# Filler projections of the last four attention phases: no bound on how early they issue, shares by key blocks at 1.25 times the even rate, and all value rows of the second pair before head 2's long blocks

## The chip, the cores and the metric

The kernel runs on one core of a Trainium2 chip. Its time is the device time of one execution in microseconds (us); lower is better. The engines that matter here are TensorE (PE, with its weight loads, PEld), VectorE (DVE), ScalarE (ACT), GpSimd (POOL) and SyncE (SP), whose queue issues every DMA of this kernel.

## What is computed

One decoder layer in fp32 on x of 1024 tokens by 1024 features. Two attention groups share an input projection: a differential group of 4 heads and a sparse group of 8 heads (compressed, selected and windowed keys, mixed by gates). Their results are concatenated, projected, added to the scaled residual and normalized; a SwiGLU feed-forward layer with a second residual and normalization follows. The part that the change concerns is the differential group:

```python
s = jnp.einsum('bqhcd,bkhcd->bhcqk', q_blk, k) * scale - slopes * dist   # c = 0, 1: two maps per head
p = masked_softmax(s, dist >= 0)                                        # causal
a = p[:, :, 0] - lam * p[:, :, 1]
o = einsum('bhqk,bkhe->bqhe', a, v)                                     # 128 columns per head
o = rms_norm(o, subln_g) * (1.0 - lam_init)
mix = concatenate([o_diff, o_nsa]) @ w_out
x = layer_norm(alpha * x + mix)
```

## The kernel before

Tokens are cut into 8 blocks of 128 (NB), features into 8 tiles of 128 (KT). Large products keep fp32 accuracy with three matmuls each (`mm3`, lines 116 to 118): high and low parts of either operand, hi*hi, hi*lo, lo*hi. A loaded weight is split into these parts by ACT (line 81) and DVE or POOL (line 83). PSUM has 8 banks: `psM` 2 for projections, `psS` 2 for scores, `psT` 3 for transposes, `psO` 1 for outputs.

A **unit** is one block of 128 queries of one head; below, d2.7 is head 2, block 7, of the differential group. `diff_units` gives each unit a `front` and a `back`. The front runs, for both maps, the scores on PE (lines 331 and 334, in pieces of at most 512 keys), a fused bias-and-minimum on DVE that takes them out of PSUM (line 340) and the exponential on ACT (line 354); then DVE (lines 475 to 478) and POOL (lines 480 and 481) combine the two maps. The back transposes the combined map on PE (line 363), copies it by ACT (line 366), multiplies by the values (line 493) and takes the block's output out by DVE and ACT (lines 497 and 498). When four blocks of a half are done, `finish` scales their rows (lines 506 to 510, with a power on POOL at 509), transposes (line 513) and stores them to `mix_d` in DRAM (line 518). Blocks 0 to 3 are a head's first half, 4 to 7 its second. Block i sees i + 1 key blocks, so blocks 4 to 7 are the long ones.

**Fillers** are projections that PE runs beside the attention, each a generator with a step for every feature tile (three matmuls): `qdf(h, hf)` and `kdf(h, hf)` project queries and keys of head h for a half of the tokens (512 columns, 24 matmuls; called QDh.hf and KDh.hf below), `dvf(pair, blocks)` the value rows of a pair of heads (256 columns, 24 matmuls for each block of 128 tokens), `out_fill(i)` the output projection of token block i (two halves of 24 matmuls in two `psM` banks). A projected query half is taken out by ACT and DVE (lines 176 and 177) into two `q` tiles of four, and three DMA moves (line 161), the third after the first two, put its parts on the other partitions. Weights stand in `w` tiles, five buffers. `wo_fill(nh)` loads half of the output weights into the buffers of x (`big` tiles, free once the projections of that half of x have run), eight loads of 256 KB with eight splits on ACT and POOL. `out_start(i)` loads the residual rows and the block's `mix_d` rows; the sparse heads' feature tiles come first in the accumulation, the differential heads' last. `held_fill` and `out_fill` thus wait for the first half of all four differential heads.

What sets the order: the program is traced once with a priority for every instruction, and a scheduler with a timeline of its own then fixes each engine's order ahead of the run; on the chip each engine takes its instructions in that order. Fillers are traced at a priority 2000 behind (`FILL_LATER`). The **planner** (line 858 on) goes through `phases`. A phase has units, fillers, `look` (how many fronts run ahead of their backs), `ahead` (a factor on the filler rate), `later` (a priority delay of the backs) and `passed`. While a back is traced, `pump` traces filler steps until the phase's `due` is reached; `share` says how much of the fillers a unit gets, from the planner's estimates of PE and DVE work in `work`. What a phase leaves over is traced in a burst at its end. With `passed` n, `proj_mm3` (line 312 on) orders each projection matmul on PE behind the first score matmul that stands n + 1 marks back in `marks`; every map of every unit sets one mark. With `None` there is no such order.

Filler order in the last four phases before, worked out from the table and the estimates: KD3.0, KD3.1, QD3.0 beside d1.7, d2.0 and d2.1; QD2.1 and value rows 4 and 5 of pair 1 beside d2.2, d2.3, d3.0, d3.1; value rows 6 and 7 and QD3.1 beside d3.2 and d3.3; output blocks 0 and 1 beside d2.4 and d2.5; output blocks 2 and 3 beside the rest. Value row 5 is traced after the front of d3.3.

Of the kernel before, what the change touches and what calls it, by code (L numbers as in the profile page):

```python
# [37 lines left out]
def layer_kernel(ctx: ExitStack, tc: tile.TileContext, xT, x, w_t, w_vg, w_dv, lam_in, subln,  # L38
# [105 lines left out]
    with ExitStack() as ctx_a:  # L144
# [238 lines left out]
        def nsa_units(p, qt, K, V):  # L383
# [7 lines left out]
            def make(i, kind):  # L391
# [55 lines left out]
                n = -(-cols // 512)  # L447
                pe = n * streamed(cols / n, 4) + streamed(P, 2 * nb + 2 * (1 - kind)) + streamed(256, 2 * nb + 1 - kind)
                dve = 2 * row_ops(width, n) + nb // 2 * 0.69 + nb % 2 * 0.42 + (0.58 if kind else 1.19)
                return front, back, (pe, dve)  # L450

            return [make(i, kind) for i in range(NB) for kind in range(2)]

# [2 lines left out]
        def diff_units(h, qt, kd, V):  # L456
# [3 lines left out]
            def make(i):  # L460
# [60 lines left out]
                n = -(-width // 512)  # L521
                pe = n * streamed(width / n, 4) + streamed(P, i + 1) + streamed(4 * P, i + 1)
                dve = 2 * row_ops(width, n) + 0.00075 * width + 1.4
                return front, back, (pe, dve)

            return [make(i) for i in range(NB)]

# [61 lines left out]
        def wo_copy(nh):  # L589
            def steps():  # L590
                for kp in range(KT // 2):
                    nc.sync.dma_start(wo_d[nh, kp], w_out[nh, kp])
                    yield 0.0
            return steps, 0.0
# [168 lines left out]
        def vg_fill(i):  # L763
            return lambda: vg_row(i, ps_m(), proj_mm3), 3.1
# [23 lines left out]
        def qf(p, hf):  # L788
            return q_fill(4 + p, hf, qn[p])

        def kf(hf):
            return k_fill(3, (), K[1], (hf,))
# [4 lines left out]
        def kdf(h, hf):  # L797
            return k_fill(9 + 2 * h, ((0, 1), (2, 4))[h % 2], kd[h], (hf,))

        def dvf(pair, blocks):  # L800
            tiles = [lambda kk: w_tiles(), lambda kk: [slot(n) for n in ((10, 11), (3, 5))[kk]]][pair]
            return dv_fill(pair, ((8, 9), (6, 7))[pair], vd[pair], blocks, tiles)
# [7 lines left out]
        def held_fill():  # L810

            def steps():
# [10 lines left out]

        phases = [
            ([(nsa, 0, (2, 1, 0, 3, 4, 5, 6, 7))],
             [vg_fill(3), vg_fill(4), qf(0, 1), vg_fill(5), vg_fill(6), vg_fill(7), qf(1, 0)], 2, 1, 80, 8),
            ([(nsa, 1, range(8))],
             [qf(1, 1), kf(0), kf(1), qf(2, 0)], 2, 1, 80, 8),
            ([(nsa, 2, range(7))],
             [qf(2, 1), wo_copy(0), dvf(0, range(8)), qf(3, 0)], 2, 1, 60, 8),  # L830
            ([(nsa, 2, (7,)), (nsa, 3, (1, 0, 2, 3, 5, 4, 6, 7))],
             [qf(3, 1), wo_copy(1), kdf(0, 0), kdf(0, 1), qdf(0, 0), kdf(1, 0)], 2, 1, 60, 8),
            ([(diff, 0, (2, 1, 0, 3, 5, 4, 6, 7))],
             [kdf(1, 1), qdf(0, 1), qdf(1, 0), dvf(1, range(4))], 1, 1, 200, 6),
            ([(diff, 1, range(8))],
             [qdf(1, 1), kdf(2, 0), qdf(2, 0), kdf(2, 1)], 1, 1, 60, 6),
            ([(diff, 2, range(4))],
             [kdf(3, 0), kdf(3, 1), qdf(3, 0)], 2, 1, 130, 6),
            ([(diff, 3, range(4))],
             [qdf(2, 1), dvf(1, (4, 5))], 2, 1, 60, 6),  # L840
            ([(diff, 2, range(4, 8))],
             [wo_fill(0), dvf(1, (6, 7)), qdf(3, 1), wo_fill(1), held_fill(), out_fill(0, False), out_fill(1, False)], 2, 1, 40, 6),
            ([(diff, 3, range(4, 8))],
             [ln_fill((0, 1)), out_fill(2, True), out_fill(3, True)], 2, 0.9, 60, 6),
        ]
        pending = []

# [7 lines left out]
                tc.cur_priority -= later  # L855
            finish_held()

        for parts, fillers, look, ahead, later, passed[0] in phases:
            units = [u for make, head, blocks in parts for u in make(head, blocks)]
            beside = [p[1] for p in pending] + [u[2] for u in units][:-look]  # L860
            given = sum(f[1] for f in fillers)
            even = (given + sum(pe for pe, _ in beside)) / sum(dve for _, dve in beside)
            share = lambda w: max(0.2, even * w[1] - w[0])
            rate = given / sum(map(share, beside)) * ahead
            queue = [(f[0], f[2] if len(f) > 2 else set()) for f in fillers]
            run = {"gen": None, "spent": 0.0, "due": 0.0}
# [422 lines left out]
```

## Time and profile before

| | |
|---|---|
| time, median of 3 runs | 1307.75 us (1307.34 to 1309.05) |
| the profiled execution's own time | 1309.7 us |
| its span | 1308.0 us, 20502 instructions |
| mean granted PE clock over the span | 0.996 |
| PE busy | 1284.6 us |
| DVE, ACT, POOL busy | 915.5, 651.1, 463.7 us |

The span runs from the first to the last instruction of that execution. The attention with its fillers takes about the first 600 us of it, the last four phases about 440 to 600 us; the feed-forward layer follows. Busy time of PE counts a matmul as long as the profile models it, so the end of one and the start of the next overlap; distances between starts tell how fast matmuls follow one another. A wait is named by the engine, the tile and the line that ended it. `psM<-slot,big` with 256 columns is a value row, `psM<-big,w` with 512 columns any other projection.

### The profile page before, as it was taken

The numbers are of one execution on the slowest core, as the hardware profiler recorded it, in microseconds if no ns is written. First come the engines' busy times: TensorE is split into PE (matmuls) and PEld (weight loads), VectorE is DVE, ScalarE is ACT, GpSimd is POOL, SyncE is SP. The second block draws the span as 40 slices with busy tenths as digits, with TensorE's granted clock in tenths as the row PEclk, the third lists the DMA queues.
The fourth block names the chain that finished last, engine by engine and source line by source line (L and its number), as shares of the span: only waits on it lengthen the run. The fifth ranks groups of instructions, "written<-read, shape, count | busy, mean of one in ns | idle before, by whom it ended". The sixth has DMA issues, their size and how long they took to land.

```text
span 1308.0 us, 20502 instructions
## 1 busy us (share of the span) xinstructions
PE 1284.6 (98%) x6955; PEld 1110.7 (85%) x6955; DVE 915.5 (70%) x1963; ACT 651.1 (50%) x1398; POOL 463.7 (35%) x499
## 2 busy tenths in 40 slices
PE   9999999999999998899999999999999999999997
PEld 7998999999899887788887888888888888888886
DVE  5577886677867564674787677776767768555588
ACT  5377877768866564653344333333233336443330
POOL 4434544444355453634623313232231322000071
PEclk9999999999999998999999999999999999999999
DMA  9411221021121324622214566655545549768541
GB/s 356 129 31 48 48 51 46 26 61 49 35 77 43 81 81 122 222 81 101 96 61 141 201 220 228 199 167 179 183 160 195 185 170 352 258 199 288 195 170 65
DMA packets 86841, 183.13 MB, mean 140 GB/s; under 512 B 10576, under 2 KB 19152, under 8 KB 86608
## 3 DMA queue, kind: packets, MB, share of 16 engines
q1 hardware_dynamic: 86736, 181.82, 42.9%
q8 instruction: 55, 0.90, 0.3%
q14 instruction: 50, 0.41, 0.1%
HBM read 116.18 MB, written 57.15 MB: 133 GB/s over the span
## 4 chain that ended last, share of the span: by engine, by line
PE 94%; DVE 2%; DMA 2%; issue 1%; ACT 0%; POOL 0%; SPq 0%; DVEq 0%; ACTq 0%; POOLq 0%
PE psM L118 11%; PE psM L116 11%; PE psM L117 11%; PE psS L118 6%; PE psS L117 6%; PE psS L116 6%; PE psT L116 5%; PE psT L118 5%; PE psT L117 5%; PE psT L373 5%; PE psS L331 4%; PE psS L334 4%; PE psO L436 2%; PE psO L434 2%; PE psO L493 2%; PE psO L118 2%
## 5 line engine op out<-in xcount | busy, mean ns | idle before, releaser
L354 ACT ACTIVATE t<-t,m 128x384 f32<-128x384 f32 (+7 forms) x192 | 144.0, 751 | 69.0 <-DVE m L340 65.2
L419 POOL TENSOR_SCALAR t<-t,r,gates 128x640 f32<-128x640 f32 (+7 forms) x128 | 99.7, 784 | 166.5 <-DVE r L413 116.7
L116 PE MATMUL psM<-big,w 128*128 128x512 f32 x304 | 120.7, 397 | 1.7 <-ACT w L81 1.7
L118 PE MATMUL psM<-big,w 128*128 128x512 f32 x304 | 119.9, 395 | 0.0
L117 PE MATMUL psM<-big,w 128*128 128x512 f32 x304 | 119.8, 394 | 0.0
L331 PE MATMUL psS<-slot,q 128*128 128x320 f32 (+10 forms) x304 | 110.9, 367 | 7.3 <-DVE m L340 4.6
L1037 POOL TENSOR_TENSOR half<-half,half 128x512 f32<-128x512 f32 x22 | 33.2, 1507 | 202.1 <-ACT half L1036 202.1
L83 DVE TENSOR_TENSOR pt<-psT,pt 128x512 fp32r<-128x512 f32 (+1 forms) x152 | 91.9, 614 | 15.5 <-ACT pt L81 14.8
L334 PE MATMUL psS<-slot,q 128*128 128x320 f32 (+10 forms) x304 | 99.2, 329 | 0.0
L81 ACT CAST pt<-psT 128x512 fp32r<-128x512 f32 (+1 forms) x152 | 77.4, 526 | 24.4 <-PE psT L373 16.5
L81 ACT CAST big<-slot 128x1024 fp32r<-128x1024 f32 (+1 forms) x54 | 54.3, 1019 | 68.8 <-DVE slot L1029 54.7
L83 DVE TENSOR_TENSOR op<-op 128x1024 fp32r<-128x1024 f32 x44 | 60.8, 1392 | 36.4 <-ACT op L81 36.0
L83 DVE TENSOR_TENSOR big<-slot,big 128x1024 fp32r<-128x1024 f32 (+1 forms) x54 | 64.0, 1191 | 29.5 <-ACT big L81 29.4
L373 PE MATMUL psT<-ident,t 128*128 128x128 f32 x528 | 83.7, 273 | 0.1
L81 ACT CAST op<-op 128x1024 fp32r<-128x1024 f32 x44 | 46.0, 1051 | 61.5 <-DMA op<-t_d 56.2
L340 DVE CUSTOM_DVE_ANT_0 t<-psS,dsel 128x384 f32<-128x384 f32 (+9 forms) x128 | 62.5, 494 | 18.3 <-PE psS L334 15.5
L1041 POOL TENSOR_TENSOR half<-half,half 128x512 f32<-128x512 f32 x22 | 36.4, 1656 | 102.8 <-DVE half L1040 102.7
L434 PE MATMUL psO<-pt,slot 128*128 128x256 f32 x264 | 72.2, 288 | 0.0
L436 PE MATMUL psO<-pt,slot 128*128 128x256 f32 x264 | 71.7, 292 | 0.0
L331 PEld LDWEIGHTS psS<-slot,q 128*128 128x128 f32 x304 | 57.7, 190 | 15.1 <-DVE m L340 9.0
L116 PEld LDWEIGHTS psM<-big,w 128*128 128x128 f32 x304 | 57.3, 188 | 11.9 <-ACT w L81 2.5
L81 ACT CAST big<-big 128x1024 fp32r<-128x1024 f32 (+1 forms) x49 | 44.4, 910 | 45.8 <-DMA big<-t_d 35.4
(371 smaller groups left out, 3973.0 us busy)
## 6 DMA issues: line engine op xcount, KB each, us to landing
a_d<-slot SPq DMA_DIRECT2D x77, 256.0 KB, 3.2
t_d<-slot SPq DMA_DIRECT2D x77, 256.0 KB, 2.2
q<-q SPq DMA_DIRECT2D x48, 256.0 KB, 2.9
slot<-in_w_up_dram SPq DMA_DIRECT2D x22, 512.0 KB, 3.9
slot<-in_w_down_dram SPq DMA_DIRECT2D x22, 512.0 KB, 4.0
op<-a_d SPq DMA_DIRECT2D x44, 256.0 KB, 3.6
op<-t_d SPq DMA_DIRECT2D x44, 256.0 KB, 4.2
big<-a_d SPq DMA_DIRECT2D x33, 256.0 KB, 3.1
```

The source lines that it names most:

```text
L81: nc.scalar.copy(hi, src)
L83: eng.tensor_sub(lo, src, hi.bitcast(F32))
L116: nc.tensor.matmul(acc, lhsT=ah, rhs=bh, start=first, stop=False, skip_group_check=more)
L117: nc.tensor.matmul(acc, lhsT=ah, rhs=bl, start=False, stop=False, skip_group_check=more)
L118: nc.tensor.matmul(acc, lhsT=al, rhs=bh, start=False, stop=last, skip_group_check=more)
L331: mm = nc.tensor.matmul(ps[:, :c + part], lhsT=q[0], rhs=k[:, ks], start=True, stop=False)
L334: nc.tensor.matmul(ps[:, :c + part], lhsT=q[1], rhs=k[:, ks], start=False, stop=True)
L354: nc.scalar.activation(t[:, :width], t[:, :width], AF.Exp, bias=m, scale=-1.0, accum_out=r)
L373: nc.tensor.transpose(tp[:rows, n * P:(n + 1) * P], s, ident)
L419: nc.gpsimd.tensor_scalar(t, t, r[:, c:c + 1], gates[:, i, gc:gc + 1], op0=ALU.mult, op1=ALU.mult)
L434: nc.tensor.matmul(po[:, :256], lhsT=v, rhs=pt[:, 0, n * 256:(n + 1) * 256], start=False, stop=False)
L436: nc.tensor.matmul(po[:, :256], lhsT=v, rhs=pt[:, 1, n * 256:(n + 1) * 256], start=False, stop=last)
```

## The change

The planner's tuple for a phase gets a seventh entry, `even`. For the first six phases it is `True` and nothing changes. For the last four it is `False`: a unit's share is then its third `work` entry, 2 i + 3 for a differential unit and so roughly its number of key blocks; units left over from the phase ahead get no share; and every unit but the last counts. `passed` is `None` there, so projection matmuls have no bound on how early they may issue. `ahead` is 1.25 in three of the four (1 before), and 0.9 in the last as before. Value rows 6 and 7 of pair 1 move from the ninth phase to the eighth, behind rows 4 and 5, and head 2's long blocks run in the order 4, 7, 6, 5. No instruction of the layer's arithmetic is added or taken away.

Worked out in the same way, the filler order after is: KD3.0 beside d2.0, KD3.1 beside d2.1, QD3.0 at the seventh phase's end; QD2.1 beside d3.0, value rows 4 and 5 beside d3.1, rows 6 and 7 at the eighth phase's end; QD3.1 and 5 of the 16 steps of output block 0 beside d2.4, then the rest of block 0 and 9 steps of block 1 beside d2.7, and the others behind.

```diff
--- before.py
+++ after.py
@@ -447,7 +447,7 @@
                 n = -(-cols // 512)
                 pe = n * streamed(cols / n, 4) + streamed(P, 2 * nb + 2 * (1 - kind)) + streamed(256, 2 * nb + 1 - kind)
                 dve = 2 * row_ops(width, n) + nb // 2 * 0.69 + nb % 2 * 0.42 + (0.58 if kind else 1.19)
-                return front, back, (pe, dve)
+                return front, back, (pe, dve, 2.0 * nb + 1)
 
             return [make(i, kind) for i in range(NB) for kind in range(2)]
 
@@ -521,7 +521,7 @@
                 n = -(-width // 512)
                 pe = n * streamed(width / n, 4) + streamed(P, i + 1) + streamed(4 * P, i + 1)
                 dve = 2 * row_ops(width, n) + 0.00075 * width + 1.4
-                return front, back, (pe, dve)
+                return front, back, (pe, dve, 2.0 * i + 3)
 
             return [make(i) for i in range(NB)]
 
@@ -823,25 +823,26 @@
 
         phases = [
             ([(nsa, 0, (2, 1, 0, 3, 4, 5, 6, 7))],
-             [vg_fill(3), vg_fill(4), qf(0, 1), vg_fill(5), vg_fill(6), vg_fill(7), qf(1, 0)], 2, 1, 80, 8),
+             [vg_fill(3), vg_fill(4), qf(0, 1), vg_fill(5), vg_fill(6), vg_fill(7), qf(1, 0)], 2, 1, 80, 8, True),
             ([(nsa, 1, range(8))],
-             [qf(1, 1), kf(0), kf(1), qf(2, 0)], 2, 1, 80, 8),
+             [qf(1, 1), kf(0), kf(1), qf(2, 0)], 2, 1, 80, 8, True),
             ([(nsa, 2, range(7))],
-             [qf(2, 1), wo_copy(0), dvf(0, range(8)), qf(3, 0)], 2, 1, 60, 8),
+             [qf(2, 1), wo_copy(0), dvf(0, range(8)), qf(3, 0)], 2, 1, 60, 8, True),
             ([(nsa, 2, (7,)), (nsa, 3, (1, 0, 2, 3, 5, 4, 6, 7))],
-             [qf(3, 1), wo_copy(1), kdf(0, 0), kdf(0, 1), qdf(0, 0), kdf(1, 0)], 2, 1, 60, 8),
+             [qf(3, 1), wo_copy(1), kdf(0, 0), kdf(0, 1), qdf(0, 0), kdf(1, 0)], 2, 1, 60, 8, True),
             ([(diff, 0, (2, 1, 0, 3, 5, 4, 6, 7))],
-             [kdf(1, 1), qdf(0, 1), qdf(1, 0), dvf(1, range(4))], 1, 1, 200, 6),
+             [kdf(1, 1), qdf(0, 1), qdf(1, 0), dvf(1, range(4))], 1, 1, 200, 6, True),
             ([(diff, 1, range(8))],
-             [qdf(1, 1), kdf(2, 0), qdf(2, 0), kdf(2, 1)], 1, 1, 60, 6),
+             [qdf(1, 1), kdf(2, 0), qdf(2, 0), kdf(2, 1)], 1, 1, 60, 6, True),
             ([(diff, 2, range(4))],
-             [kdf(3, 0), kdf(3, 1), qdf(3, 0)], 2, 1, 130, 6),
+             [kdf(3, 0), kdf(3, 1), qdf(3, 0)], 2, 1.25, 130, None, False),
             ([(diff, 3, range(4))],
-             [qdf(2, 1), dvf(1, (4, 5))], 2, 1, 60, 6),
-            ([(diff, 2, range(4, 8))],
-             [wo_fill(0), dvf(1, (6, 7)), qdf(3, 1), wo_fill(1), held_fill(), out_fill(0, False), out_fill(1, False)], 2, 1, 40, 6),
+             [qdf(2, 1), dvf(1, range(4, 8))], 2, 1.25, 60, None, False),
+            ([(diff, 2, (4, 7, 6, 5))],
+             [wo_fill(0), qdf(3, 1), wo_fill(1), held_fill(), out_fill(0, False), out_fill(1, False)],
+             2, 1.25, 40, None, False),
             ([(diff, 3, range(4, 8))],
-             [ln_fill((0, 1)), out_fill(2, True), out_fill(3, True)], 2, 0.9, 60, 6),
+             [ln_fill((0, 1)), out_fill(2, True), out_fill(3, True)], 2, 0.9, 60, None, False),
         ]
         pending = []
 
@@ -855,12 +856,16 @@
                 tc.cur_priority -= later
             finish_held()
 
-        for parts, fillers, look, ahead, later, passed[0] in phases:
+        for parts, fillers, look, ahead, later, passed[0], even in phases:
             units = [u for make, head, blocks in parts for u in make(head, blocks)]
-            beside = [p[1] for p in pending] + [u[2] for u in units][:-look]
             given = sum(f[1] for f in fillers)
-            even = (given + sum(pe for pe, _ in beside)) / sum(dve for _, dve in beside)
-            share = lambda w: max(0.2, even * w[1] - w[0])
+            if even:
+                beside = [p[1] for p in pending] + [u[2] for u in units][:-look]
+                ratio = (given + sum(w[0] for w in beside)) / sum(w[1] for w in beside)
+            else:
+                pending = [(p[0], (0, 0, 0)) for p in pending]
+                beside = [u[2] for u in units][:-1]
+            share = lambda w: max(0.2, ratio * w[1] - w[0]) if even else w[2]
             rate = given / sum(map(share, beside)) * ahead
             queue = [(f[0], f[2] if len(f) > 2 else set()) for f in fillers]
             run = {"gen": None, "spent": 0.0, "due": 0.0}
```

## Rows read from the trace of the kernel before

**Rows 1.** The page, part 1: busy us, share of the span and instructions of an engine.

```profile
PE 1284.6 (98%) x6955; PEld 1110.7 (85%) x6955; DVE 915.5 (70%) x1963; ACT 651.1 (50%) x1398; POOL 463.7 (35%) x499
```

**Rows 2.** The page, part 2: PE's busy share in 40 equal slices of 32.7 us, in tenths.

```profile
PE   9999999999999998899999999999999999999997
```

**Rows 3.** Windows: start and end of the stretch and its length in us, then busy us and instructions (x) of PE, PEld, DVE, ACT and POOL, the granted PE clock, the share of the DMA engines that was busy, and GB/s.

```profile
495.00:500.00 5.00, 3.92 (x34) 3.72 (x32) 3.46 (x11) 2.95 (x9) 3.94 (x4) 1.00 1.00 224
500.00:515.00 15.00, 10.75 (x65) 10.19 (x66) 4.28 (x17) 5.04 (x18) 2.06 (x5) 0.77 0.54 138
535.00:560.00 25.00, 20.47 (x116) 15.93 (x116) 18.59 (x56) 16.78 (x41) 16.29 (x15) 1.00 0.43 120
```

**Rows 4.** Waits of PE from 420 to 600 us: engine, tile and line that waited, who ended the wait, us in total, times, longest us.

```profile
PE psS L331 <- DVE m L340: 3.2, 6, 1.5
PE psT L513 <- DVE od L510: 3.0, 1, 3.0
PE psS L331 <- DMA q<-q: 2.3, 1, 2.3
PE psM L116 <- ACT w L81: 1.7, 1, 1.7
```

**Rows 5.** The chain that ended last, in order of time, in two stretches (493 to 509 and 549 to 557 us): start us, us, what.

```profile
494.55 6.51 DMA q<-q
501.13 6.59 DMA q<-q
507.77 0.33 PE psS L331
...
549.07 3.28 DMA mix_d<-tmp
552.37 3.57 DMA w<-mix_d
556.63 0.50 PE psM L116
```

**Rows 6.** Timeline of PE from 474 to 512 us: start us, us, engine, line, operation, tiles and forms, count, and in brackets the idle time before it with what ended it. Of the value row that starts at 495.59 the first and the last of its 24 matmuls; of the projection matmuls from 509.47 to 511.81 the first and the last of 12.

```profile
474.65 0.82 PE L363 MATMUL psT<-ident,t 128*128 128x128 f32 x6
...
495.59 0.36 PE L116 MATMUL psM<-slot,big 128*128 128x256 f32 x1
...
498.41 0.28 PE L118 MATMUL psM<-slot,big 128*128 128x256 f32 x1
...
502.38 2.21 PE L363 MATMUL psT<-ident,t 128*128 128x128 f32 x9
...
508.05 0.27 PE L331 MATMUL psS<-slot,q 128*128 128x128 f32 x1
...
508.27 0.33 PE L116 MATMUL psM<-slot,big 128*128 128x256 f32 x1
...
509.47 0.41 PE L116 MATMUL psM<-slot,big 128*128 128x256 f32 x1
...
511.81 0.41 PE L118 MATMUL psM<-slot,big 128*128 128x256 f32 x1
```

**Rows 7.** Timelines of POOL and PE from 455 to 477 us, the same columns: two weight splits on POOL, a score piece of d1.6, and the first matmuls of two projections.

```profile
455.12 2.54 POOL L83 TENSOR_TENSOR w<-w 128x512 fp32r<-128x512 f32 x2 [6.25 <-ACT w L81]
...
473.15 2.52 POOL L83 TENSOR_TENSOR w<-w 128x512 fp32r<-128x512 f32 x2 [2.43 <-ACT w L81]
...
457.93 0.37 PE L334 MATMUL psS<-slot,q 128*128 128x448 f32 x1
458.13 0.39 PE L116 MATMUL psM<-big,w 128*128 128x512 f32 x1
458.36 0.39 PE L117 MATMUL psM<-big,w 128*128 128x512 f32 x1
...
476.77 0.39 PE L116 MATMUL psM<-big,w 128*128 128x512 f32 x1
```

**Rows 8.** Timeline of PE from 519 to 523 us, the same columns: the last scores of d3.3, and the last of the 18 value-row matmuls behind them.

```profile
519.57 0.39 PE L331 MATMUL psS<-slot,q 128*128 128x512 f32 x1
...
...
522.28 0.28 PE L118 MATMUL psM<-slot,big 128*128 128x256 f32 x1
```

**Rows 9.** Groups of instructions from 425 to 600 us, shapes kept apart: line, engine, operation, tiles, forms, count, then busy us, mean ns of one, and the idle time before them. The form with `m` is the second piece of a row of scores.

```profile
L340 DVE CUSTOM_DVE_ANT_0 t<-psS,dsel 128x512 f32<-128x512 f32 x12 | 8.1, 684 | 3.0 <-PE psS L334 2.1 <-PE psT L363 0.9
L340 DVE CUSTOM_DVE_ANT_0 t<-psS,dsel 128x384 f32<-128x384 f32 x12 | 6.6, 554 | 4.4 <-PE psS L334 4.3
L340 DVE CUSTOM_DVE_ANT_0 t<-psS,dsel,m 128x512 f32<-128x512 f32 x6 | 4.5, 748 | 0.3 <-PE psS L334 0.2
L340 DVE CUSTOM_DVE_ANT_0 t<-psS,dsel,m 128x384 f32<-128x384 f32 x6 | 3.7, 616 | 1.4 <-PE psS L334 1.0
```

**Rows 10.** Waits of the SP queue from 440 to 600 us, columns as in rows 4; L99 are the loads of output weights and `mix_d` rows.

```profile
SPq L99 <- PE psM L118: 27.1, 10, 10.5
```

**Rows 11.** Timeline of POOL from 535 to 545 us, columns as in rows 6: splits of the output weights, a combine, and the power of head 3's first row scaling.

```profile
535.41 7.93 POOL L83 TENSOR_TENSOR big<-big 128x512 fp32r<-128x512 f32 x6
543.33 1.00 POOL L480 TENSOR_SCALAR t<-t,r 128x288 f32<-128x288 f32 x1
544.30 1.04 POOL L509 TENSOR_TENSOR ss<-ss,mhalf 128x4 f32<-128x4 f32 x1
```

**Rows 12.** The page, part 6: DMA issues of the whole span, count, KB each, median us from issue to landing.

```profile
q<-q SPq DMA_DIRECT2D x48, 256.0 KB, 2.9
```

## The prediction

> **What bounds the kernel now.** I read the page's busy shares first: TensorE (PE) is busy 98% of the span, VectorE 70% [rows 1]. So time can only be won where PE stands still or runs slowly, and the slices show where: outside the span's end the PE line falls below 9 in two slices only, from 491 to 556 us [rows 2]. That is where the last four phases run. Windows then give the size. In stretch S1 (495 to 515 us) PE is busy 3.92 of 5 and 10.75 of 15 us, so it idles 1.08 + 4.25 = 5.33 us, and the granted clock is 0.77 from 500 us on. In stretch S2 (535 to 560 us) it idles 25.00 - 20.47 = 4.53 us, at full clock [rows 3]. Everything the change can win outright lies in these two.
>
> Then the waits name what ended each stop: 3.0 us for `od` (the row scaling of L510), 2.3 us for the moves `q<-q`, 3.2 us in six waits for L340, 1.7 us for a `w` tile that ACT casts [rows 4]. The chain in order of time joins them. S1: the two serial moves of a query half take 6.51 and 6.59 us, and PE's scores at 507.77 wait for them. S2: `mix_d<-tmp` takes 3.28 us, `w<-mix_d` 3.57 us, and only then, at 556.63, do the output-projection matmuls go on [rows 5].
>
> The PE timeline says why nothing filled S1. A value-row projection (24 matmuls of 128x256) starts at 495.59, its last matmul at 498.41. The next row starts at 508.27, directly behind the scores of d3.0 (head 3, block 0) at 507.77 [rows 6]. By the code this is the bound: value row 5 of pair 1 is traced after the front of d3.3, and the bound of 6 places each of its matmuls behind the score mark seven marks back, which is d3.0's second. So ready work stood in PE's in-order queue behind scores that waited for DMA. I take that bound, not the sharing rule, as the cause of S1.
>
> **The change, part by part.** Part 1, no bound. It removes a placement rule, no instruction. Cover that it frees in S1: value rows 5, 6 and 7 of pair 1, 72 matmuls. Start to start they take (498.41 - 495.59) / 23 = 0.123 us [rows 6], so 72 x 0.123 = 8.8 us of work for 5.33 us of idle time. Nothing else holds them: their weights are loaded before, and each needs one `psM` bank and one ACT copy. Nor does the bound's end let the earlier projections run away. KD3.0 (key half 0 of head 3) starts at 458.13, right behind the weight split on POOL that ends at 455.12 + 2.54 = 457.66, and QD3.0 starts at 476.77, behind the split that ends at 473.15 + 2.52 = 475.67 [rows 7]. Those splits wait for the five `w` buffers, which stay as they are. I cost the earlier fillers at nothing: weights, not the bound, time them.
>
> With the idle time goes the slow clock. After waits of 3.00 and 2.33 us, 12 projection matmuls from 509.47 to 511.81 stand 2.34 / 11 = 0.213 us apart, against 0.123 [rows 6]: the lower of the two clock levels, 1.2 GHz. Some 13 matmuls x 0.09 = 1.2 us; nine transposes at 502.38 take 2.21 us, against 0.82 for six, so some 1.1 for nine, at 474.65 [rows 6]: up to 1.1 us more, part of which may be a wait for `psT`. So 1.2 to 2.3 us, and I take 1.8. S1 gives 5.3 + 1.8 = 7.1 us (6.5 to 7.6).
>
> Part 2, the emptier stretch after. Between the last scores of d3.3 at 519.57 [rows 8] and 556.63 the fillers in before were 18 value-row matmuls (2.2 us), QD3.1 (24 matmuls 0.23 us apart [rows 7], 5.5 us) and half of the first output block (24 matmuls, 5.5 us): 13.2 us. Used up in S1, the 18 are gone from here: S2 grows by 0 to 2.2 us. Zero if the 8.8 - 5.3 = 3.5 us that S1 doesn't need stay for later; all if the scheduler issues them as soon as it can. I take the middle, 1.1.
>
> Part 3, the unit order 4, 7, 6, 5. Its reader is head 3's first row scaling (finish of d3.0 to d3.3), traced behind the back of d2.4, and so now behind the fronts of blocks 4, 7 and 6 instead of 4, 5 and 6. d2.7 in place of d2.5 costs DVE 2 x ((0.684 - 0.554) + (0.748 - 0.616)) = 0.52 us in L340 [rows 9]: 0.5 us later on the chain that ends S2. ACT's exponentials grow beside it and are hidden by DVE's. Total work is equal; the short block comes last, where PE has output blocks to run.
>
> Part 4, the rate (1.25) and the key-block shares. They change where a filler is traced, not when it may run: fillers carry a priority 2000 behind, and KD3.0, traced in the back of d1.7, ran at 458.13, between the score pieces of d1.6 (448 columns) [rows 7]. Worked out from the table, after traces KD3.0 one unit later, value rows 6 and 7 in a burst at the end of the eighth phase, QD3.1 and 5 of 16 steps of the first output block in the back of d2.4. I cost this at nothing; if trace order did decide, value rows 6 and 7 would still precede d2.4.
>
> Part 5, what the moved steps bring along. Value rows 6 and 7: an ACT copy each, no DMA, so on SP they pass nothing. QD3.1: an ACT and a DVE copy of its half, and three `q<-q` moves on SP, which sit in order with the `wo_d` loads; SP waits 27.1 us in all for the x tiles that these loads overwrite [rows 10]. Its reader d3.4 comes behind head 2's four long blocks, so a late move is covered; without that cover the two serial moves cost what they cost in S1. The `wo_d` loads of the second half follow QD3.1, with eight subtractions on POOL; in before six of them fill 535.41 to 543.33, and the combine of 1.00 us that they held up stands in front of the `ss` power of that row scaling, at 544.30 [rows 11]. QD3.1 earlier moves them out of the way: 0 to 1.0 us off S2, taken as 0.5.
>
> Sum: -7.1 + 1.1 + 0.5 - 0.5 = -6.0 us. The profiled execution took 1309.7 us (span 1308.0), 1.95 above the median of 1307.75; the same saving gives 1303.7 for a like profile and **1301.8 us** for the median. By the bounds, -7.6 + 0 + 0.5 - 1.0 = -8.1 (1299.7) to -6.5 + 2.2 + 0.5 = -3.8 (1304.0).
>
> **The rivals.** (a) Better: S2 closes as well, since QD3.1, the `wo_d` loads and the first output half all come some 5 to 8 us sooner while PE works through the long fronts. That adds up to 4.5 us: 1297.3. For it: DVE is busy 18.59 of S2's 25 us [rows 3], so it has room. Against: S2's end is a DMA chain behind a DVE chain, and each is serial.
>
> (b) No change: transfers collide. The `wo_d` loads of the second half and the x rows now fall nearer the row scaling's `mix_d` write and read. In S1 the moves took 6.51 and 6.59 us beside such loads, at a DMA share of 1.00 just before [rows 3, 5], against a median of 2.9 us over the span [rows 12]. Were `mix_d<-tmp` and `w<-mix_d` to take 6.55 each instead of 3.28 and 3.57, S2 grows by 6.25: 1308.0. Against: in S2 both found a freer queue, and the loads may be over by then. The Trainium skill ("DMA: Bandwidth & Descriptors", section "Issuing engines are not separate DMA queues") says that transfers from any engine run on the same 16 DMA engines and interleave; by that rule loads moved earlier slow whatever waits beside them, as the trace bears out with the 6.5 us moves.
>
> (c) Slower: the cover is spent too early. With no bound, if value rows 5 to 7 and QD3.1 are all through before d3.3's last scores, S2 has 5.5 of its 13.2 us of fillers left. The idle time there grows by 7.7 instead of 1.1, to 4.53 + 7.7 + 0.5 - 0.5 = 12.2 us, and at S1's ratio of clock loss to idle time (1.8 / 5.33 = 0.34) that is 4.1 us more: -7.1 + 7.7 + 0.5 - 0.5 + 4.1 = +4.7, 1312.5. It decides once S2's idle time exceeds its old 4.53 by more than 7.1 / 1.34 = 5.3 us. For it: nothing but buffers restrains a filler now. Against: QD3.1 can't leave its `psM` bank before d3.3's scores have released the `q` tiles, the value rows share the other bank, and S2's early part has attention of its own.
>
> (d) The change doesn't do what it says: the order of PE's queue is made ahead, and if the scheduler put the rows where it put them before, S1 stays: 1307.75. Value row 5's start directly behind the scores speaks against it.
>
> **How the numbers follow.** Forecast 0.45, (a) 0.20, (b) 0.13, (c) 0.15, (d) 0.07. What a measurement of this kernel can tell from no change is about 0.2%, 2.6 us: under 1305.1 is faster, over 1310.4 slower. Faster: 0.45 + 0.20 and a little of (b) = 0.66; same: the rest of (b), (d) = 0.18, with a sliver of (c); slower 0.16. The range reaches from just beyond (a), 1296.5, to 1310.0, past (b) and (d), and leaves most of (c) out.
>
> **What would show it.** S1: value-row matmuls before d3.0's first scores, no PE wait of over 1 us for `q<-q` or `od`, granted clock 1.00 throughout. Part 2: few or no value-row matmuls between d3.3's scores and the output block's second half. Part 3: the L508 of head 3's first scaling behind two fronts with 512-column score pieces. (b) shows in landing times of `mix_d<-tmp` and `w<-mix_d` over 6 us, (c) in a PE window below 3 us of 5 with a clock under 1.00 before the first output block resumes. The forecast fails if the idle time between 440 and 600 us doesn't fall, wherever it then stands.

## The result, and the profile after

The changed kernel takes **1299.09 us** (median of 4 runs, 1298.14 to 1299.55) against 1308.40 for the kernel before beside it (4 runs, 1307.34 to 1309.18): ratio 0.9928 [0.9911, 0.9946] (in brackets the 95% interval, here and below), 9.3 us less. The forecast was 1301.8 (1296.5 to 1310.0), which is 6.0 us less than 1307.75. The profiled execution took 1298.14 us, the lowest of the four, where the one of before took 1309.7, so the two traces lie further apart (11.6 us) than the medians.

The page of the kernel after, parts 1 and 2, to be held against [rows 1, 2]: the span, PE's busy time and PE's slices.

```profile
span 1296.4 us, 20500 instructions
PE 1279.8 (99%) x6955; PEld 1108.3 (85%) x6955; DVE 915.7 (71%) x1963; ACT 651.2 (50%) x1398; POOL 464.5 (36%) x499
PE   9999999999999999999999999999999999999997
```

The two slices of before that were below 9 are full, with the same 6955 matmuls. Windows of the kernel after, with the columns of [rows 3]: first the two stretches that made up S1, then the whole of the last four phases.

```profile
495.00:500.00 5.00, 4.50 (x38) 4.33 (x38) 3.57 (x14) 2.50 (x9) 2.62 (x3) 1.00 0.93 282
500.00:515.00 15.00, 15.00 (x121) 14.64 (x120) 9.26 (x38) 8.36 (x30) 4.46 (x9) 1.00 0.42 113
440.00:600.00 160.00, 156.36 (x932) 136.98 (x931) 101.13 (x275) 87.98 (x224) 81.37 (x77) 1.00 0.41 126
```

The same view of the kernel before, for the whole of the last four phases:

```profile
440.00:600.00 160.00, 149.57 (x875) 129.74 (x874) 97.05 (x267) 86.11 (x220) 74.21 (x72) 0.98 0.39 114
```

S1 has 0.50 us of idle time left (it had 5.33) and the granted clock is 1.00 throughout (it was 0.77). Between 440 and 600 us the idle time falls from 10.43 to 3.64 us, by 6.8. In the whole span it falls by 6.8 too (1308.0 - 1284.6 = 23.4, 1296.4 - 1279.8 = 16.6), so outside these phases PE idles as long as before. The other 4.8 us between the two spans are busy time, for the same 6955 matmuls; the mean granted clock was 0.996 before and is 0.999 after.

The PE waits of the kernel after from 420 to 600 us, columns of [rows 4]:

```profile
PE psS L331 <- DVE m L340: 1.1, 1, 1.1
PE psT L513 <- DVE r L475: 1.1, 1, 1.1
PE psS L331 <- DVE od L497: 0.5, 1, 0.5
PE psO L493 <- ACT ms L498: 0.5, 1, 0.5
```

The waits for `q<-q` (2.3 us) and for `od` of L510 (3.0) are gone. PE's timeline after, columns of [rows 6], shows what stands where they stood: d3.0's first scores, the transposes that wait for `od`, the last scores of d3.3, the first and the last of the value-row matmuls behind these, and the output block's second half.

```profile
495.84 0.30 PE L331 MATMUL psS<-slot,q 128*128 128x128 f32 x1 [0.50 <-DVE od L497]
...
501.94 0.60 PE L513 MATMUL psT<-ident,od 128*128 128x128 f32 x4
...
507.16 0.48 PE L331 MATMUL psS<-slot,q 128*128 128x512 f32 x1
...
507.70 0.28 PE L118 MATMUL psM<-slot,big 128*128 128x256 f32 x1
...
514.36 0.28 PE L118 MATMUL psM<-slot,big 128*128 128x256 f32 x1
...
546.80 0.39 PE L116 MATMUL psM<-big,w 128*128 128x512 f32 x1
```

I had expected 72 value-row matmuls to go **into a gap** ahead of d3.0's scores. Instead there is no gap: the scores come at 495.84, 11.9 us earlier than 507.77 [rows 5], and by 495.84 only 3 value-row matmuls have run. 34 of the 96 are still to come behind d3.3's last scores (507.70 to 514.36), where before had 18 [rows 8].

The wait for `od` shows the same. Before, DVE's L510 ends at 501.77 and the transposes start at 501.91, after 3.0 idle us. After, L510 ends at 500.17, 1.6 us earlier, but the transposes start at 501.94, no earlier than before. What has gone is the standing still: the first scores of d3.0 and d3.1 and 41 value-row matmuls now fill PE from 495.84 on.

The scores could come earlier because the query half that d3.0 reads, QD3.0, was there earlier. ACT's timelines show when the two query halves were taken out of PSUM; in either kernel the first row is QD3.0 and the second QD2.1. Before:

```profile
492.48 0.69 ACT L176 ACTIVATE q<-psM,qscale 128x512 fp32r<-128x512 f32 x1 [1.26 <-PE psM L118]
493.91 0.68 ACT L176 ACTIVATE q<-psM,qscale 128x512 fp32r<-128x512 f32 x1
```

After:

```profile
486.10 0.69 ACT L176 ACTIVATE q<-psM,qscale 128x512 fp32r<-128x512 f32 x1
493.06 0.68 ACT L176 ACTIVATE q<-psM,qscale 128x512 fp32r<-128x512 f32 x1
```

QD3.0 is 6.4 us earlier, QD2.1 hardly. The 24 + 24 matmuls of the two halves run in about the same place in both kernels, but not in the same order. In before's order on PE, 19 of QD3.0 are followed by 15 of QD2.1, and QD3.0's last five stand in turn with QD2.1's next. Its last one is the 43rd of the 48. Each projection goes through L116, L117 and L118 in turn, so the two can be told apart where they mix. Of these lines of before the first, third and fifth are QD3.0's (its 20th, 21st and last matmul), the other two QD2.1's:

```profile
490.21 0.39 PE L117 MATMUL psM<-big,w 128*128 128x512 f32 x1
490.45 0.40 PE L116 MATMUL psM<-big,w 128*128 128x512 f32 x1
490.68 0.39 PE L118 MATMUL psM<-big,w 128*128 128x512 f32 x1
490.91 0.40 PE L117 MATMUL psM<-big,w 128*128 128x512 f32 x1
...
492.05 0.39 PE L118 MATMUL psM<-big,w 128*128 128x512 f32 x1
```

In the kernel after, all 24 of QD3.0 come first. What follows on the SP queue (start us, us, what, count): first before, then after.

```profile
494.03 1.10 SPq L161 DMA_DIRECT2D q<-q  x2
495.23 2.23 SPq L608 DMA_DIRECT2D slot<-in_x_dram  x2
497.56 9.88 SPq L161 DMA_DIRECT2D q<-q  x4
```

```profile
488.56 4.68 SPq L161 DMA_DIRECT2D q<-q  x3
493.33 0.53 SPq L99 DMA_DIRECT2D w<-mix_d  x1
494.35 1.23 SPq L608 DMA_DIRECT2D slot<-in_x_dram  x2
495.67 8.72 SPq L161 DMA_DIRECT2D q<-q  x3
```

After, the three moves of QD3.0 are all issued ahead of the two loads of residual rows (512 KB each by their tile) and of QD2.1's moves. Before, QD3.0's first two moves are under way together with those loads (the DMA engines are fully busy from 495 to 500 us [rows 3]), and its third is issued together with QD2.1's.

### The profile page after: what moved, and what is told of

It is laid out like the page before. It is cut to its first block, busy times and chain, and to the rows that moved or that the text cites. A ratio compares the mean times of both kernels' runs of the same rounds, so it can differ in the third digit from the quotient of the medians.

```text
span 1296.4 us, 20500 instructions
## 1 busy us (share of the span) xinstructions
PE 1279.8 (99%) x6955; PEld 1108.3 (85%) x6955; DVE 915.7 (71%) x1963; ACT 651.2 (50%) x1398; POOL 464.5 (36%) x499
## 4 chain that ended last, share of the span: by engine, by line
PE 94%; DVE 3%; issue 1%; ACT 1%; DMA 0%; POOL 0%; DVEq 0%; ACTq 0%; POOLq 0%
PE psM L116 11%; PE psM L118 11%; PE psM L117 11%; PE psS L118 6%; PE psS L117 6%; PE psS L116 6%; PE psT L116 5%; PE psT L118 5%; PE psT L117 5%; PE psT L373 5%; PE psS L331 4%; PE psS L334 3%; PE psO L436 2%; PE psO L434 2%; PE psO L493 2%; PE psO L118 2%
## 5 line engine op out<-in xcount | busy, mean ns | idle before, releaser
L116 PE MATMUL psM<-big,w 128*128 128x512 f32 x304 | 120.3, 396 | 0.4 <-DVE slot L171 0.3
L118 PE MATMUL psM<-big,w 128*128 128x512 f32 x304 | 119.9, 395 | 0.0
L117 PE MATMUL psM<-big,w 128*128 128x512 f32 x304 | 119.6, 394 | 0.0
L81 ACT CAST big<-slot 128x1024 fp32r<-128x1024 f32 (+1 forms) x54 | 54.2, 1018 | 67.5 <-DVE slot L1034 53.6
L118 PEld LDWEIGHTS psM<-big,w 128*128 128x128 f32 x304 | 57.1, 188 | 11.5
L116 PEld LDWEIGHTS psM<-big,w 128*128 128x128 f32 x304 | 57.3, 188 | 10.7 <-DVE slot L171 0.4
```

The lines of the kernel that those rows point to most:

```text
L81: nc.scalar.copy(hi, src)
L116: nc.tensor.matmul(acc, lhsT=ah, rhs=bh, start=first, stop=False, skip_group_check=more)
L117: nc.tensor.matmul(acc, lhsT=ah, rhs=bl, start=False, stop=False, skip_group_check=more)
L118: nc.tensor.matmul(acc, lhsT=al, rhs=bh, start=False, stop=last, skip_group_check=more)
```

## The experiments

Each kernel ran in five rounds against the kernel before (1308.76, 1309.13 or 1309.64 us, the median of 20 to 25 runs, in the three groups below).

**First group: which part carries the gain?** The theory was the prediction's, that the bound makes S1. The rival was that shares and rate matter. e1 takes the bound of the last four phases out of the kernel before and does nothing else (one of the four lines):

```diff
-             [kdf(3, 0), kdf(3, 1), qdf(3, 0)], 2, 1, 130, 6),
+             [kdf(3, 0), kdf(3, 1), qdf(3, 0)], 2, 1, 130, None),
...
```

> The kernel before with the bound alone taken off in the last four phases; old shares, old rates, value rows 6 and 7 and the unit order as before. Theory (the bound held value rows 5 to 7 behind d3.0's scores): nearly all of the 9.3 us come, 1299 to 1301 us, value-row matmuls stand ahead of d3.0's first scores, the granted clock stays at 1.00 from 500 to 515 us. Rival (the shares by key blocks and the earlier rows are what helps): 1306 us or more.

Measured: 1305.08, ratio 0.9966 [0.9955, 0.9977], under half of the gain. Idle time from 440 to 600 us is 6.28 us. QD3.0 is taken out at 491.54, d3.0's scores come at 505.30, and PE still waits 1.7 us for `q<-q`. (The eleven runs of e1 reach from 1302.55 to 1307.63; the profiled execution took 1303.03, so its trace shows less than the median loses.) The rows do go where I had put them, 59 of their matmuls between 495.11 and the scores, but they then lack further on: from 525 to 550 us PE idles 3.60 us, against 2.85 in the kernel after.

e2 is the changed kernel with the bound put back in the same four:

```diff
-             [kdf(3, 0), kdf(3, 1), qdf(3, 0)], 2, 1.25, 130, None, False),
+             [kdf(3, 0), kdf(3, 1), qdf(3, 0)], 2, 1.25, 130, 6, False),
...
```

> The changed kernel with the bound of 6 back in the last four phases; shares, rates, rows and unit order as changed. Theory: value row 4 too is now traced behind the front of d3.3 and so bound behind d3.0's second score, so up to 24 more matmuls (2.9 us) are missing where PE waits for d3.0's query moves: 1309 to 1314 us, slower than before. Rival (shares, rate and row order carry the gain): 1299 to 1302 us.

Measured: 1310.99, 1.0016 [1.0007, 1.0024]. The time is as expected, but the stop is another one: PE waits 3.8 us for ACT's `tmp`, and in the chain ACT stands behind a cast that waits for an output-weight load of 8.07 us (491.95). The value rows start at 507.85, behind d3.0's scores (505.57), as in before. QD3.0 is out at 492.55 here although it runs ahead of QD2.1: with the bound, the projections ahead of it are late already, KD3.0 starting at 463.10 where it starts at 456.22 in the kernel after.

e3 keeps all of the change but the shares and the rate (one of three lines; in the last phase only `even` changes):

```diff
-             [kdf(3, 0), kdf(3, 1), qdf(3, 0)], 2, 1.25, 130, None, False),
+             [kdf(3, 0), kdf(3, 1), qdf(3, 0)], 2, 1, 130, None, True),
...
```

> The changed kernel with the old share rule and rates (1 instead of 1.25) in the last four phases; no bound, rows and unit order as changed. Theory: where a filler is traced hardly matters once nothing bounds it, 1297 to 1302 us, within 0.2% of the changed kernel. Rival (the shares matter): 1303 us or more.

Measured: 1306.37, 0.9976 [0.9966, 0.9986]. This refutes the theory that the shares cost and bring nothing: QD3.0 comes at 492.88 and the SP queue has the order of before.

e4 is the changed kernel with head 2's long blocks in the old order:

```diff
-            ([(diff, 2, (4, 7, 6, 5))],
+            ([(diff, 2, range(4, 8))],
```

> The changed kernel with head 2's long blocks in the order 4, 5, 6, 7 again. Theory: the order costs the first row scaling of head 3 some 0.5 us of VectorE work, so without it 1298 to 1299.5 us, within 0.2%. Rival (the order with block 7 early gives part of the gain, as its long front runs while fillers are left): 1301 to 1304 us.

Measured: 1299.15, 0.9923 [0.9911, 0.9935]. The order is worth nothing that can be measured.

**Second group: is it QD3.0's place?** The new theory comes from the planner. A back of the seventh phase is traced at a priority delay of 130 (`later`), one of the eighth at 60, and the filler steps that `pump` traces inside a back carry its delay on top of their 2000. In before, QD3.0's last steps are traced in such backs with 130, and QD2.1's behind them with 60, so the scheduler takes QD2.1's first. With the new shares QD3.0 is traced in the burst at the phase's end, outside any back and without the 130. e9 gives that burst a delay in the changed kernel, and nothing else:

```diff
+            tc.cur_priority += 260 if later == 130 else 0
             while step():
                 pass
+            tc.cur_priority -= 260 if later == 130 else 0
```

> The changed kernel, but the steps of QD3.0 (and all else that the seventh phase leaves for its end) are traced 260 priority places later, so that QD2.1 overtakes QD3.0 again. New theory (what counts is that QD3.0, traced in the phase's end and so without the back's delay of 130, is finished before QD2.1, some 6 us sooner; with it the output weights and d3.0's query moves): 1303 to 1307 us, ACT takes QD3.0 out at about 492 us instead of 486, and PE waits for the moves again. First theory (the missing bound alone): 1298 to 1300.5 us.

Measured: 1310.37, 1.0005 [0.9997, 1.0014]. The whole gain is gone, more than expected, with no bound, all rows at hand and the new shares. The chain of e9 (start us, us, what):

```profile
495.67 7.86 DMA q<-q
...
503.55 5.81 DMA q<-q
...
509.40 0.33 PE psS L331
```

And windows of e9:

```profile
495.00:505.00 10.00, 10.00 (x85) 9.84 (x83) 3.53 (x11) 3.98 (x13) 5.09 (x5) 1.00 1.00 227
504.00:510.00 6.00, 1.76 (x17) 1.52 (x15) 0.12 (x1) 1.75 (x5) 0.00 (x0) 1.00 0.58 118
525.00:550.00 25.00, 20.94 (x103) 16.16 (x102) 19.59 (x59) 15.67 (x40) 18.14 (x17) 0.86 0.36 95
```

Here the value rows do what I had predicted of them: PE is fully busy from 495 to 505, with 72 of their matmuls from 495.18 on. The moves take 7.86 and 5.81 us, the scores come at 509.40, and PE stands still for 4.2 us behind the rows. The last row matmul starts at 515.65, and later, from 525 to 550 us, 4.06 us are idle at a granted clock of 0.86 (2.85 us at 1.00 in the same stretch of the kernel after). That is the mechanism of rival (c), cover spent too early, but not its size: from d3.3's last scores to the output block's second half (523.45 to 559.90 us) e9 idles 4.90 us at a granted clock of 0.91, where (c) had 12.2 us.

e11 is the other direction, the kernel **before**, bound and shares and all, with the delay of 130 taken off the filler steps alone:

```diff
             def pump(part, work):
+                cut = later if later == 130 else 0
+                tc.cur_priority -= cut
                 while run["spent"] < run["due"] + part * share(work) * rate and step():
                     pass
+                tc.cur_priority += cut
```

> The kernel before with its bound, and the seventh phase's fillers traced without the back's delay of 130 places. New theory: QD3.0 leaves first, d3.0's scores come before 500 us, so the bound on value row 5 costs little: 1300 to 1304 us. First theory (the bound is what stops PE): 1306 to 1309 us.

Measured: 1300.27, 0.9933 [0.9920, 0.9945]: within the intervals as fast as the whole change. The chain of e11:

```profile
493.01 4.39 DMA q<-q
497.45 2.92 DMA q<-q
...
500.50 0.30 PE psS L331
```

QD3.0 is out at 490.66, less than two microseconds earlier than in before, but its moves take 7.3 us in place of 13.1 [rows 5]. Of the 7.3 us by which d3.0's scores come earlier, 1.5 are the earlier start of the first move and 5.8 the shorter moves.

e10 has the same edit on top of e1, so no bound either (`pump` as above):

```diff
+                tc.cur_priority -= cut
...
+                tc.cur_priority += cut
```

> The kernel before without the bound in the last four phases, old shares and rates, and with one more edit: the seventh phase's fillers are traced without the back's delay of 130 places. New theory: as the changed kernel, 1298 to 1301 us. First theory (shares and priority don't matter): 1304 to 1306 us, as with the bound alone taken off.

Measured: 1299.38, 0.9924 [0.9910, 0.9937], with no wait for `q<-q` at all.

e5 takes the bound out of the eighth phase alone, where value row 5 is traced:

```diff
-             [qdf(2, 1), dvf(1, (4, 5))], 2, 1, 60, 6),
+             [qdf(2, 1), dvf(1, (4, 5))], 2, 1, 60, None),
```

> The kernel before with the bound taken off in the eighth phase alone (QD2.1 and value rows 4 and 5). First theory: value row 5 comes free, but rows 6 and 7 stay bound behind the front of d3.1 and d3.2: 24 of 72 matmuls, 2.9 us of cover, 1304 to 1306 us. New theory (QD2.1 unbound can now overtake QD3.0 more easily, which costs what the cover brings): 1306 to 1309 us.

Measured: 1306.97, 0.9982 [0.9973, 0.9991]. PE waits 4.0 us for `q<-q`; QD3.0 is out at 492.23, as in before. The time lies where the new theory put it, but QD2.1 overtaking more easily is not seen.

**Third group: the cause made small, and the rest.** e13 changes one number of the kernel before, so that backs of the seventh phase and their fillers have the delay of the eighth:

```diff
-             [kdf(3, 0), kdf(3, 1), qdf(3, 0)], 2, 1, 130, 6),
+             [kdf(3, 0), kdf(3, 1), qdf(3, 0)], 2, 1, 60, 6),
```

> The kernel before with one number changed: the back's delay in the seventh phase is 60 instead of 130. Bound, shares, rates, rows and order as before. New theory: QD3.0 then goes ahead of QD2.1 and nearly the whole gain comes, 1299 to 1302.5 us. Rival (the bound or the shares are needed as well): 1304 us or more.

Measured: 1301.71, 0.9937 [0.9923, 0.9952]. In its order on PE all 24 matmuls of QD3.0 stand ahead of QD2.1's. QD3.0 is out at 488.58. Its chain:

```profile
490.59 3.74 DMA q<-q
494.38 2.93 DMA q<-q
...
497.45 0.30 PE psS L331
```

e12 asks how much of the moves' length is the two loads of residual rows. In the kernel before, SP issues them behind QD3.0's third move (`third[0]`; the lines that keep that move, and those for the other blocks, are left out):

```diff
-            nc.sync.dma_start(acc[i], x[i * P:(i + 1) * P, :])
+            if i < 2:
+                with tc.issue_after(third[0].ins):
+                    nc.sync.dma_start(acc[i], x[i * P:(i + 1) * P, :])
...
```

> The kernel before, with one order added on SP: the two loads of residual rows (512 KB each) are issued behind the third query move of QD3.0 instead of ahead of it. It parts the two halves of the new theory, that QD3.0 ends late and that its moves are slow beside those loads. If the loads make up half of the wait: the moves take 3 to 5 us each instead of 6.5, d3.0's scores come at 500 to 504 us, 1303 to 1306.5 us. If only QD3.0's late end matters: 1307 to 1309.5 us.

Measured: 1308.25, 0.9985 [0.9976, 0.9994]. Its chain:

```profile
494.35 5.79 DMA q<-q
500.21 3.20 DMA q<-q
503.45 0.47 PE psS L333
```

The last move is as short as one in a free stretch, the first two are not: QD2.1's moves now go beside them. The scores come 4.3 us earlier, yet 1.4 us are gained, since PE idles 4.74 us of the 20 from 495 to 515 us, little less than before, at a clock of 0.83. With QD3.0 out at 492.28 the loads alone explain little. No run puts QD2.1's moves behind as well while QD3.0 stays late, so how much of the loss is the late end of QD3.0's matmuls and how much the order of the moves on SP is not separated. The delay decides both.

e6 puts value rows 6 and 7 and the unit order back where they were in before, with all else changed:

```diff
-             [qdf(2, 1), dvf(1, range(4, 8))], 2, 1.25, 60, None, False),
-            ([(diff, 2, (4, 7, 6, 5))],
-             [wo_fill(0), qdf(3, 1), wo_fill(1), held_fill(), out_fill(0, False), out_fill(1, False)],
+             [qdf(2, 1), dvf(1, (4, 5))], 2, 1.25, 60, None, False),
+            ([(diff, 2, range(4, 8))],
+             [wo_fill(0), dvf(1, (6, 7)), qdf(3, 1), wo_fill(1), held_fill(), out_fill(0, False), out_fill(1, False)],
```

> The changed kernel with value rows 6 and 7 back in the ninth phase, and head 2's long blocks in the order 4, 5, 6, 7, which that needs; shares, rates and no bound as changed. New theory: QD3.0 still goes ahead, so 1298 to 1301 us. Rival (all value rows ahead of the long units are needed): 1302.5 us or more.

Measured: 1299.83, 0.9919 [0.9906, 0.9932]: the rows' place is worth nothing that can be measured. e8 takes the bound out of the first six phases as well, in the hope of more (one of six lines):

```diff
-             [qf(1, 1), kf(0), kf(1), qf(2, 0)], 2, 1, 80, 8, True),
+             [qf(1, 1), kf(0), kf(1), qf(2, 0)], 2, 1, 80, None, True),
...
```

> The changed kernel with no bound in the first six phases either; a try for a faster version. In those phases TensorE idles 2.3 us in all from 100 to 440 us, so at most some 2 us can come: 1297 to 1300 us. If fillers are then used up early and TensorE runs dry before the phases end: 1302 us or more.

Measured: 1313.07, 1.0026 [1.0017, 1.0035], some 13 us (0.98%) over the changed kernel. Windows of the six early phases, e8 first, then the kernel after:

```profile
100.00:440.00 340.00, 334.58 (x2237) 300.12 (x2236) 244.49 (x860) 241.67 (x648) 152.02 (x209) 1.00 0.18 46
```

```profile
100.00:440.00 340.00, 337.76 (x2316) 312.46 (x2315) 254.77 (x882) 249.78 (x670) 161.94 (x219) 1.00 0.20 51
```

In the same 340 us e8 gets 79 matmuls fewer done, at full clock, and its idle time there is only 3.2 us longer. Over the whole span PE counts 1292.6 us of busy time in e8 against 1279.8 for the same 6955 matmuls. Part of the 79 may be another mix of shapes in these 340 us, the 12.8 us of busy time can't be. So most of the loss lies inside what counts as busy, and which instruction waits there was not found: this stays open. In the early phases the bound is worth having.

The runs that change only the last four phases, ordered by when QD3.0 leaves PSUM (ACT, L176). The idle time is that of PE from 440 to 600 us:

| kernel | QD3.0 out, us | d3.0's first scores | PE idle, us | ratio |
|---|---|---|---|---|
| e9, changed, burst delayed | 493.07 | 509.40 | 9.42 | 1.0005 |
| e3, changed, old shares | 492.88 | 507.40 | 7.09 | 0.9976 |
| e2, changed, bound kept | 492.55 | 505.57 | 9.20 | 1.0016 |
| before | 492.48 | 507.77 | 10.43 | 1 |
| e12, before, loads later | 492.28 | 503.45 | 9.18 | 0.9985 |
| e5, before, 8th phase unbound | 492.23 | 507.74 | 8.34 | 0.9982 |
| e1, before, unbound | 491.54 | 505.30 | 6.28 | 0.9966 |
| e11, before, no 130 on fillers | 490.66 | 500.50 | 4.32 | 0.9933 |
| e13, before, 60 for 130 | 488.58 | 497.45 | 4.59 | 0.9937 |
| e4, changed, old unit order | 487.51 | 496.93 | 3.57 | 0.9923 |
| e10, unbound, no 130 on fillers | 487.36 | 497.08 | 2.68 | 0.9924 |
| e6, changed, rows back | 486.93 | 496.50 | 2.43 | 0.9919 |
| after | 486.10 | 495.84 | 3.64 | 0.9928 |

The step lies between 491.54 and 490.66, where the three moves come clear of the loads and of QD2.1's moves: in e1 the loads are issued at 494.49, between QD3.0's second and third move, in e11 at 498.63, behind all three. With QD3.0 late, the bound, the rows' place and the loads spread the ratio from 0.9966 to 1.0016; with it early, the intervals of all six kernels overlap. No version is measurably faster than the changed kernel.

## Why the prediction was right, and where it was not

The time came out 2.7 us below the forecast and inside its range, and the place was right: S1 closes, the clock there is 1.00, and the idle time between 440 and 600 us falls. **The step that failed** is "I take that bound, not the sharing rule, as the cause of S1", and with it "I cost this at nothing" of part 4. Ready rows did stand behind the scores, but what made the scores late was that QD2.1 went ahead of QD3.0's last matmuls, so that QD3.0's moves went beside the loads and QD2.1's. The bound alone is worth 0.34% of the 0.72% (e1); undoing only the late query half, with the bound kept, is worth 0.67% (e11) or 0.63% (e13); and with no bound but a late query half nothing is left (e9). I had read one side effect of the shares rightly, that QD3.0 is traced "at the seventh phase's end", and argued it away with the 2000 that all fillers carry. The delay of the back, 130 or 60, comes on top of that 2000 and decides between two fillers.

What in the profile could have said so: the moves of 6.51 and 6.59 us against a median of 2.9 [rows 5, 12] stood in the text as evidence for rival (b), while S1's cost was sought in what could fill the wait. That a wait can be covered doesn't make the cover's absence its cause.

**Term by term.** Two pairs of windows run between the same marks in either kernel: the end of QD2.1's matmuls, d3.3's last scores, and the output block's second half. Before:

```profile
493.30:519.50 26.20, 20.87 (x146) 19.89 (x145) 11.91 (x39) 11.45 (x37) 7.84 (x11) 0.87 0.56 141
519.50:556.60 37.10, 32.60 (x191) 26.76 (x190) 24.06 (x73) 22.89 (x57) 22.91 (x21) 1.00 0.65 205
```

After:

```profile
492.55:507.10 14.55, 14.05 (x114) 13.62 (x113) 10.46 (x38) 8.78 (x28) 6.22 (x10) 1.00 0.67 175
507.10:546.75 39.65, 36.80 (x235) 32.10 (x234) 26.98 (x82) 26.57 (x69) 24.09 (x22) 1.00 0.60 194
```

- S1, idle time: 5.33 to 0.50 us, so 4.8 of the 5.3 forecast.
- S1, clock: the two stretches together shrink from 63.3 to 54.2 us, by 9.1, for the same filler work (96 value-row and 48 wider projection matmuls) and 12 matmuls more of the attention (349 against 337 in all). Idle time explains 4.83 + 1.65 = 6.5 of it; the 2.6 left I put down to the clock, which was 0.87 over the first stretch and is 1.00 now. No run measured this part by itself. I took 1.8 and had 2.3 as the upper bound. So S1 gives some 7.4 where I had 7.1, for another reason.
- S2: I forecast 1.1 us more, and its idle time went from 4.50 to 2.85 instead. The rows were not spent in a gap, as there is none, so 34 instead of 18 of their matmuls are left for the stretch behind d3.3's scores. As a whole S2 is 2.55 us longer, with 235 matmuls in it against 191: of the 44 more, 32 had stood in S1 and 12 behind S2. Rival (a) came true by about a third (1.65 us of its 4.5).
- The terms of 0.5 us for the unit order and the earlier output weights: e4 shows the order at nothing that can be measured. The weights' part was not measured by itself.
- "I cost the earlier fillers at nothing: weights, not the bound, time them": KD3.0 starts at 456.22 instead of 458.13, and at 456.64 in e1, where the bound alone is gone. So the bound did hold it. The mark ahead of S1 comes 0.75 us earlier (492.55 for 493.30), a small gain that I did not see.
- Together 0.75 + 9.1 of the 11.6 us between the two traces lie ahead of the output block's second half. The last 1.75 lie behind it, where 12 matmuls fewer are left.

The chain of the kernel after in what was S2, for [rows 5, 11]: it is one of compute engines, and the output block's second half comes at 546.80, not 556.63.

```profile
535.73 1.65 POOL t L480
537.38 1.01 POOL ss L509
538.42 1.39 DVE od L510
539.96 0.64 PE psT L513 x4
```

Rival (b) did not come: S2 closes further, and no `mix_d` transfer stands in that chain. Rival (c) did not come in the changed kernel. e9 shows its mechanism, at less than half of the idle time that it was priced at (4.90 us for 12.2): once QD3.0 is late and nothing holds the rows, they are used up, PE idles 4.24 us in front of d3.0's scores all the same, and further on it idles more than in the kernel after (4.90 us for 2.85 between like marks). That the sum held although its reason failed was luck: both reasons price the same thing, the idle time in S1 and the clock that goes with it. Filling the gap got half of that (e1); not letting it arise got nearly all (e11).

QD3.0's two serial moves take 13.1 us beside loads and the other half's moves, 9.0 with the loads put behind (e12), and 6.7 with both behind (e13). That agrees with the rule of the Trainium skill that the prediction cited ("DMA: Bandwidth & Descriptors", section "Issuing engines are not separate DMA queues"), by which DMAs run on the same 16 DMA engines and interleave. SP issues every DMA of this kernel, so no run here shows the rule's part on several issuing engines.

## What to carry to other kernels

When an engine waits for a transfer, first ask why that transfer is late and long, by following its data back to the instruction that produced it and comparing its length with the median of its kind; only then ask what could fill the wait. Where several parts change at once, undo each alone and also build the suspected cause alone in the old kernel: here one number (130 to 60) gives most of what four edits give, and two of the four give nothing. In a program that a scheduler orders by priority, a delay meant for one kind of work is inherited by whatever is traced inside it.

## What the runs showed of the hardware that was not expected

- What a 256 KB move runs beside mattered more here than a microsecond or two of its start. QD3.0 out 1.8 us earlier (e11 for before) makes d3.0's scores 7.3 us earlier, as the same pair of moves takes 7.3 us instead of 13.1.
- More ready work did not help where what is waited for came late: in e9 PE is fully busy for ten microseconds and then stands still for 4.2, and the 24 row matmuls that are left are gone before the next thin stretch, where the clock falls to 0.86.
- PE's busy share can hide a loss. e8 has 99% on the page and takes some 13 us longer, with 12.8 us more of "busy" for the same matmuls. Matmuls counted in a fixed window (2237 against 2316) show what the share doesn't.
